# Whole-array matmuls for two heads at a time: values with 128 stationary columns, rotary keys on 128 rows

## The chip, the core and the metric

One core of a Trainium2 chip runs the whole program. The metric is the device time of one execution in microseconds. Five engines work side by side, each through its own queue in order: TensorE (PE; its weight loads are listed apart as PEld), VectorE (DVE), ScalarE (ACT), GpSimd (POOL) and SyncE (SP, which issues most DMAs). Matmul results land in PSUM, from where DVE and ACT read them.

## The reference, cut to what matters

Two blocks follow each other on 512 tokens of width 1024. The first block has two layers; each projects its input, runs three kinds of attention and projects back. The second has one layer with three mixers, then a feed-forward network. Four head groups matter here:

```python
# first block, per layer: forgetting heads (4 of width 64), stick-breaking heads (4 of width 64)
logits = s + cqb[..., :, None] - cum_logf[..., None, :]
p = jax.nn.softmax(jnp.where(causal, logits, -jnp.inf), axis=-1)
return jnp.einsum('bhqk,bhkd->bhqd', p.astype(v.dtype), v)
...
weights = jnp.where(strict, jnp.exp(jax.nn.log_sigmoid(z) + after), 0.0)
return jnp.einsum('bhqk,bhkd->bhqd', weights.astype(v.dtype), v)
...
yb = _from_blocks(ob) * jax.nn.silu(bg)      # and yc likewise

# second block: latent attention (4 heads; 128 plain and 64 rotary dimensions)
s = (jnp.einsum('bthd,bshd->bhts', qn, k_nope)
     + jnp.einsum('bthr,bsr->bhts', qp, k_pe)).astype(jnp.float32) * scale
```

The rotary keys `k_pe` are the same for all four heads.

## The kernel before, in words

A Python program writes all instructions; a scheduler then orders each engine's queue by priority. Side work (attention) and main work (projections of the next stage, with their weights loaded, split into two parts and multiplied three times in `mm3`, L212) are interleaved: a generator of attention steps is advanced some steps for each step of the projections (`merge`, L85). Attention steps have raised priority (`ahead`), their transposes and value matmuls lowered (`lag`).

Heads of width 64 are kept in pairs, `pr`, head `hh` of a pair on partitions 0 to 63 or 64 to 127. Projections leave 128 rows, two heads, in one tile; values `v[k]` hold, for key block k, 128 tokens on the rows and all heads' values side by side as columns, so the two heads of a pair are 128 adjacent columns.

Forgetting attention (`att_b`, L737) runs over pairs, then query blocks i of 128 (so i+1 key blocks), then the two heads. Each step makes scores, a masked minimum (`masked`, L720), an exponential and a scaling (`softmax`), and hands the rest to `step` (L1081) and the class `Steps`: one step later the weights are transposed on PE and copied by ACT, another step later `put` multiplies values and weights, one matmul group over the key blocks with the head's 64 value columns stationary and the 128 query columns moving, onto the head's 64 rows of the PSUM tile `pv`. `pv` has one buffer for the whole kernel (`PS`, L82); one tile serves a pair, and when both heads and all blocks are in it, `out_bc` (L558) multiplies it into the pair's gate with one DVE operation (L562).

Stick-breaking attention (`att_c`, L792) takes the heads in turn: `front` makes scores and logarithms, `sums` walks the key blocks from the last to the first and its `put` (L841) multiplies, with 64 value columns stationary and then 128 to 512 query columns moving (L847, L851). Again one `pv` serves a pair and one DVE operation (L564) takes it out.

Latent attention (`mla`, L1362) runs over query blocks and four heads. A score is a 128-row matmul (L1372) plus a rotary one (L1373) over 64 rows: queries of two heads lie on one tile's two halves, and the rotated keys `kpe`, made on rows 0 to 63 at L1220, are copied to rows 64 to 127 (L1221), so that each head finds keys on its own rows. In that part of the program tiles of 2 KB a row come from a set of 24 (`slot`, L67).

In the trace float32 matmuls stand as two instructions each, one after the other.

Of the kernel before, what the change touches and what calls it, by code (L numbers as in the profile page):

```python
# [15 lines left out]
ALU = mybir.AluOpType  # L16
# [4 lines left out]
P = 128  # L21
S = 512
NT = S // P
# [11 lines left out]
class Net:  # L35
# [471 lines left out]
    def layer1(self, l, hT, post, nxt):  # L507
# [5 lines left out]
        v, lf = self.vl  # L513
# [41 lines left out]

        oo, wait, last = {}, [], []

        def out_bc(k, pv, scale):  # L558

            g = gates[k]  # L560
            if scale == 1.0:
                nc.vector.tensor_mul(g, pv, g)  # L562
            else:
                nc.vector.scalar_tensor_tensor(g, pv, scale, g, op0=ALU.mult, op1=ALU.mult)  # L564
            finish(k, g)

        def finish(k=None, o=None):

# [168 lines left out]
    def att_b(self, bq, bk, v, lf, out, slot):  # L737
        nc = self.nc

        x = lf[:, :, 0:4]  # L740
        e = self.u("lfe", [P, NT, 4], 1)
        nc.scalar.activation(e, x, AF.Abs)
        nc.scalar.activation(e, e, AF.Exp, scale=-1.0)
        nc.scalar.activation(e, e, AF.Ln, bias=1.0)
        nc.vector.scalar_tensor_tensor(x, x, 0.0, e, op0=ALU.min, op1=ALU.subtract)
        nc.vector.tensor_copy(lf[:, :, 4:8], x)
        if not self.bounds:
            self.hgrn_bounds()
        nc.vector.tensor_copy(lf[:, :, 8:16], lf[:, :, 0:8])
        cumr = self.wa()  # L750
        nc.gpsimd.memset(cumr, 1.0)
        nc.gpsimd.affine_select(cumr, cumr, pattern=[[1, S]], compare_op=ALU.is_ge,
                                fill=0.0, base=0, channel_multiplier=-1)
        cum = self.p("s")
        for j in range(NT):
            nc.tensor.matmul(cum[0:16, j * P:], lhsT=lf[:, j, :], rhs=cumr[:, :S - j * P],
                             start=j == 0, stop=j == NT - 1)

        C, cu = self.sub.tile([P, S], F32R, name=self.nm("g"), tag="g", bufs=4), cum[0:16]
        nc.gpsimd.memset(C.bitcast(F32), 0.0)  # L760
        up = self.wa(dt=F32R)[0:16]
        sel = lambda k: self.sel[:, k:k + 1]
        nc.scalar.copy(up, cu)
        x = self.wa()[0:16]
        nc.vector.tensor_scalar_mul(x, up, sel(0))
        nc.vector.scalar_tensor_tensor(C[0:16], cu, sel(1), x, op0=ALU.mult, op1=ALU.add)
        yield
        steps = Steps(self)
        for pr in range(2):
            pv = self.p("pv")  # L770
            for i in range(NT):
                w = (i + 1) * P
                qi = slice(i * P, w)
                for hh in range(2):
                    h, r = pr * 2 + hh, hh * 64
                    sc = self.p("s")

                    n = max(w, 256)
                    self.dots(sc[:, :n], bq[pr][hh], bk[pr], hh, qi, slice(0, n))
                    scored = nc.tensor.matmul(sc[:, :n], lhsT=self.pick[:, h, :], rhs=C[:, :n], start=False, stop=True)  # L780
                    st = self.t("st", [P, 4], 6)
                    p = self.wa()
                    self.masked(p, sc, w, st[:, 1:2])
                    nc.scalar.activation(p[:, :w], p[:, :w], AF.Exp, bias=st[:, 1:2], scale=-1.0, accum_out=st[:, 2:3])
                    self.softmax(p, st, 0.5, w)
                    self.step(steps, scored, p, i, pv[r:r + 64, qi], lambda k, h=h: v[k][:, 512 + h * 64:576 + h * 64],
                              done=(lambda pr=pr, pv=pv: out(4 + pr, pv, 1.0)) if i == NT - 1 and hh else None)
                    yield
        steps.end()
        yield  # L790

    def att_c(self, cq, ck, v, out):  # L792
# [31 lines left out]
        pvs, puts = {}, []  # L824

        def sums(pr, hh, z, hi, lo):
            h, r = pr * 2 + hh, hh * 64
            for k in range(NT - 1, -1, -1):
                w = S - k * P

                sc = self.p("s")
                todo = [(self.ntri if j == k else self.nones, j, y) for j in range(k, NT) for y in (hi, lo)]
                for n, (m, j, y) in enumerate(todo):
                    wj = max(S - j * P, 256)
                    end = 128 + co[j] + S - j * P
                    last = nc.tensor.matmul(sc[:, S - wj:], lhsT=m, rhs=y[:, end - wj:end], start=n == 0, stop=n == len(todo) - 1)  # L836
                p = z[:, co[k]:co[k] + w]
                nc.vector.tensor_add(p, sc[:, k * P:], p)
                nc.scalar.activation(p, p, AF.Exp)

                def put(after, k=k, p=p, w=w):  # L841
                    if hh == 0 and k == NT - 1:
                        pvs[pr] = self.p("pv")
                    pv = pvs[pr]
                    vv = v[k][:, 768 + h * 64:832 + h * 64]
                    with self.lag():
                        x = nc.tensor.matmul(pv[r:r + 64, k * P:(k + 1) * P], lhsT=vv, rhs=p[:, :P], start=k == NT - 1, stop=False)  # L847
                        if after:
                            self.after(x, after)
                        if k < NT - 1:  # L850
                            nc.tensor.matmul(pv[r:r + 64, (k + 1) * P:], lhsT=vv, rhs=p[:, P:], start=False, stop=k == 0)  # L851
                    if hh and k == 0:
                        out(6 + pr, pv, 0.5)

                puts.append(put)
                if len(puts) > 1:
                    puts.pop(0)(last)
                yield
# [279 lines left out]
    def attention2(self, hT):  # L1138
# [67 lines left out]
        with self.tp("ph2m", "left") as mid:  # L1206
# [3 lines left out]
            with self.tp("ph2b", "right") as self.sub:  # L1210
# [7 lines left out]
                self.run_all(main((plist, "aq", 0, aq, -P ** -0.5), (plist, "aq", 256, aq, -P ** -0.5)))  # L1218
                self.run_all(low.second(qn, qp, kn, vc, tab, mslot))
                kpe = self.rope2_apply(kpr, 64, tab, self.slot())  # L1220
                nc.scalar.copy(kpe[64:128], kpe[0:64])  # L1221
            mxp = self.ctx2.enter_context(self.tp("ph2c", "right"))
            mx = [mxp.tile([P, S], F32, name=f"mx{c}", tag="mx", bufs=8) for c in range(8)]
            with self.tp("ph2d", "right") as self.sub:
# [137 lines left out]
    def mla(self, qn, qp, kn, kpe, vc, out):  # L1362
        nc = self.nc
        steps = Steps(self)
        for i in range(NT):
# [1 line left out]
            qi = slice(i * P, w)  # L1367
            pv = self.p("pv", [P, 4, P])
            for h in range(4):
                r = (h % 2) * 64  # L1370
                sc = self.p("s")
                nc.tensor.matmul(sc[:, :w], lhsT=qn[h][:, qi], rhs=kn[h][:, :w], start=True, stop=False)  # L1372
                scored = nc.tensor.matmul(sc[:, :w], lhsT=qp[h // 2][r:r + 64, qi], rhs=kpe[r:r + 64, :w], start=False, stop=True)  # L1373
                st = self.t("st", [P, 4], 6)
                p = self.wa()
                self.masked(p, sc, w, st[:, 1:2])
                nc.scalar.activation(p[:, :w], p[:, :w], AF.Exp, bias=st[:, 1:2], scale=-1.0, accum_out=st[:, 2:3])
                self.softmax(p, st, 0.5, w)
                self.step(steps, scored, p, i, pv[:, h, :], lambda k, h=h: vc[k][:, h * P:(h + 1) * P],
                          done=(lambda qi=qi, pv=pv: self.split_heads(out, qi, pv)) if h == 3 else None)  # L1380
                yield
# [448 lines left out]
```

## Time and profile before

| | |
|---|---|
| median of 3 runs | 1677.36 us (1676.02 to 1679.92) |
| the profiled execution | 1676.82 us |
| its span, first to last instruction | 1675.1 us |
| TensorE busy | 1618.9 us, 97% |
| VectorE busy | 1056.8 us, 63% |
| ScalarE busy | 734.6 us, 44% |
| GpSimd busy | 105.7 us, 6% |
| mean granted TensorE clock | 0.995 |

A row of the page's first part is an engine, its busy time, share of the span and number of instructions. Busy time of PE includes modelled ends, and its matmuls overlap: what one matmul costs is read from the start of one to the start of the next. A form such as `128*64 128x128` is rows by columns of the stationary operand, then the size of the moving one.

### The profile page before, as it was taken

The numbers are of one execution on the slowest core, as the hardware profiler recorded it, in microseconds if no ns is written. First come the engines' busy times: TensorE is split into PE (matmuls) and PEld (weight loads), VectorE is DVE, ScalarE is ACT, GpSimd is POOL, SyncE is SP. The second block draws the span as 40 slices with busy tenths as digits, with TensorE's granted clock in tenths as the row PEclk, the third lists the DMA queues.
The fourth block names the chain that finished last, engine by engine and source line by source line (L and its number), as shares of the span: only waits on it lengthen the run. The fifth ranks groups of instructions, "written<-read, shape, count | busy, mean of one in ns | idle before, by whom it ended". The sixth has DMA issues, their size and how long they took to land.

```text
span 1675.1 us, 24263 instructions
## 1 busy us (share of the span) xinstructions
PE 1618.9 (97%) x9320; PEld 1374.6 (82%) x9320; DVE 1056.8 (63%) x2281; ACT 734.6 (44%) x1507; POOL 105.7 (6%) x131
## 2 busy tenths in 40 slices
PE   6999999999999999899889999999999999999997
PEld 6878797987787889787778866788889988888997
DVE  7686779784578796747999995624355444343233
ACT  4455664443465643465443765522233222222222
POOL 1021000000000000002221001100000000000000
PEclk9999999999999999999999999999999999999999
DMA  7453032341121414332011320223432533333321
GB/s 229 141 167 109 26 116 74 101 152 51 51 76 39 148 55 126 121 100 64 26 30 49 93 76 27 91 91 108 144 120 101 176 101 101 101 101 95 95 90 62
DMA packets 141883, 160.06 MB, mean 96 GB/s; under 512 B 14100, under 2 KB 131108, under 8 KB 141256
## 3 DMA queue, kind: packets, MB, share of 16 engines
q1 hardware_dynamic: 135960, 141.34, 28.0%
q0 software_dynamic: 2944, 11.86, 2.1%
q10 hardware_dynamic: 2864, 5.32, 1.0%
q8 instruction: 73, 1.20, 0.3%
q14 instruction: 42, 0.34, 0.1%
HBM read 143.55 MB, written 15.21 MB: 95 GB/s over the span
## 4 chain that ended last, share of the span: by engine, by line
PE 76%; DVE 13%; ACT 3%; issue 2%; DMA 1%; POOL 1%; ACTq 0%; POOLq 0%
PE pj L217 18%; PE pj L218 18%; PE pj L216 18%; PE pv L1093 3%; PE s L216 2%; PE s L217 2%; PE s L218 2%; PE tr L731 2%; DVE wlo L203 2%; PE s L717 1%; PE s L836 1%; PE s L718 1%; DVE ixs L1313 1%; DMA wraw<-in_w_in_dram 1%; ACT whi L202 1%
## 5 line engine op out<-in xcount | busy, mean ns | idle before, releaser
L216 PE MATMUL pj<-hTh,whi 128*128 128x512 f32 (+1 forms) x1136 | 440.5, 388 | 0.0
L217 PE MATMUL pj<-hTl,whi 128*128 128x512 f32 (+1 forms) x1136 | 440.3, 388 | 0.0
L218 PE MATMUL pj<-hTh,wlo 128*128 128x512 f32 (+1 forms) x1136 | 439.8, 388 | 0.3 <-DVE wlo L203 0.3
L203 DVE TENSOR_TENSOR wlo<-wraw,whi 128x1024 fp32r<-128x1024 f32 (+3 forms) x237 | 271.9, 1153 | 240.1 <-ACT whi L202 236.3
L202 ACT CAST whi<-wraw 128x1024 fp32r<-128x1024 f32 (+3 forms) x237 | 229.1, 980 | 327.1 <-PE pj L217 193.5
L216 PEld LDWEIGHTS pj<-hTh,whi 128*128 128x128 f32 x1136 | 213.6, 188 | 45.4 <-issue 6.6
L217 PEld LDWEIGHTS pj<-hTl,whi 128*128 128x128 f32 x1136 | 213.6, 188 | 43.4 <-issue 4.7
L218 PEld LDWEIGHTS pj<-hTh,wlo 128*128 128x128 f32 x1136 | 213.6, 188 | 43.2 <-issue 3.8
L216 PE MATMUL pj<-whi,hTh 128*128 128x256 f32 (+2 forms) x352 | 101.1, 289 | 3.4 <-ACT whi L207 2.7
L218 PE MATMUL pj<-whi,hTl 128*128 128x256 f32 (+2 forms) x352 | 102.5, 292 | 0.0
L217 PE MATMUL pj<-wlo,hTh 128*128 128x256 f32 (+2 forms) x352 | 101.2, 288 | 0.0
L217 PE MATMUL pj<-wlo,t2k 128*128 128x256 f32 x304 | 85.9, 283 | 0.0
L218 PE MATMUL pj<-whi,t2k 128*128 128x256 f32 x304 | 85.7, 282 | 0.0
L216 PE MATMUL pj<-whi,t2k 128*128 128x256 f32 x304 | 85.3, 281 | 0.0
L216 PE MATMUL s<-whi,t2k 128*128 128x256 f32 x264 | 73.8, 280 | 0.0
L218 PE MATMUL s<-whi,t2k 128*128 128x256 f32 x264 | 73.8, 280 | 0.0
L217 PE MATMUL s<-wlo,t2k 128*128 128x256 f32 x264 | 73.8, 280 | 0.0
L216 PEld LDWEIGHTS pj<-whi,hTh 128*128 128x128 f32 x352 | 68.2, 194 | 5.1 <-ACT whi L207 3.3
L217 PEld LDWEIGHTS pj<-wlo,hTh 128*128 128x128 f32 x352 | 68.4, 194 | 0.5 <-DVE wlo L203 0.2
L218 PEld LDWEIGHTS pj<-whi,hTl 128*128 128x128 f32 x352 | 68.3, 194 | 0.4
L734 ACT COPY wa<-tr 128x128 f32<-128x128 f32 (+3 forms) x96 | 40.7, 424 | 58.8 <-PE tr L731 57.4
L722 DVE CUSTOM_DVE_ANT_0 wa<-s,mask 128x128 f32<-128x128 f32 (+3 forms) x112 | 52.5, 485 | 11.4 <-PE tr L731 7.9
(455 smaller groups left out, 3120.2 us busy)
## 6 DMA issues: line engine op xcount, KB each, us to landing
wraw<-in_w_in_dram SPq DMA_DIRECT2D x112, 512.0 KB, 3.8
wraw<-in_w_ffn_gate_dram SPq DMA_DIRECT2D x22, 512.0 KB, 3.9
wraw<-in_w_ffn_up_dram SPq DMA_DIRECT2D x22, 512.0 KB, 4.6
wraw<-in_w_ffn_down_dram SPq DMA_DIRECT2D x16, 512.0 KB, 3.6
tok<-hres SPq DMA_DIRECT2D x12, 512.0 KB, 7.7
wraw<-in_w_out_dram SPq DMA_DIRECT2D x12, 512.0 KB, 4.3
hres<-tok SPq DMA_DIRECT2D x12, 512.0 KB, 2.7
wraw<-in_w_out_dram SPq DMA_DIRECT2D x8, 384.0 KB, 3.0
```

What stands on the lines that cost most here:

```text
L202: nc.scalar.copy(hi[:, ka:kb], raw)
L203: nc.vector.tensor_sub(lo[:, ka:kb], raw, hi[:, ka:kb])
L216: nc.tensor.matmul(out, lhsT=wh(k), rhs=xh(k), start=start and k == 0, stop=False)
L217: nc.tensor.matmul(out, lhsT=wh(k), rhs=xl(k), start=False, stop=False)
L218: nc.tensor.matmul(out, lhsT=wl(k), rhs=xh(k), start=False, stop=stop and k == nk - 1)
L717: nc.tensor.matmul(sc, lhsT=stacked[:, rows], rhs=twice[hh][:, cols], start=True, stop=False)
L718: return nc.tensor.matmul(sc, lhsT=stacked[:, rows], rhs=twice[2 + hh][:, cols], start=False, stop=stop)
L722: self.nc.vector.tensor_tensor_reduce(p[:, :w], sc[:, :w], self.maskw[:, S - w:] if mask is None else mask, scale=1.0, scalar=3e38, op0=AL ...
L731: x = nc.tensor.transpose(pt[:, j, :], src[:, j * P:(j + 1) * P], self.ident)
L734: nc.scalar.copy(dst[:, :n, :], pt[:, :n, :])
L836: last = nc.tensor.matmul(sc[:, S - wj:], lhsT=m, rhs=y[:, end - wj:end], start=n == 0, stop=n == len(todo) - 1)
L1093: x = self.nc.tensor.matmul(out, lhsT=l, rhs=r, start=k == 0, stop=k == i)
```

## The change

Values: the 64-column stationary operand becomes the 128 columns of the pair, for each head. The result then has 128 rows, of which the head's own 64 are kept. Because both heads now write all rows, each head has a `pv` tile of its own: the loop of forgetting attention runs heads outside and query blocks inside, and `out_bc` is called per head on its 64 rows; the pair is finished after the second.

Rotary keys: two tiles in place of one, the keys on rows 0 to 63 with zeros below, and the keys on rows 64 to 127 with zeros above; the rotary matmul takes all 128 rows of the queries' tile, so the other head's queries meet zeros.

```diff
-        def out_bc(k, pv, scale):
+        def out_bc(k, hh, pv, scale):
 
-            g = gates[k]
+            r = slice(hh * 64, hh * 64 + 64)
+            g = gates[k][r]
             if scale == 1.0:
-                nc.vector.tensor_mul(g, pv, g)
+                nc.vector.tensor_mul(g, pv[r], g)
             else:
-                nc.vector.scalar_tensor_tensor(g, pv, scale, g, op0=ALU.mult, op1=ALU.mult)
-            finish(k, g)
+                nc.vector.scalar_tensor_tensor(g, pv[r], scale, g, op0=ALU.mult, op1=ALU.mult)
+            if hh:
+                finish(k, gates[k])
...
         for pr in range(2):
-            pv = self.p("pv")
-            for i in range(NT):
-                w = (i + 1) * P
-                qi = slice(i * P, w)
-                for hh in range(2):
-                    h, r = pr * 2 + hh, hh * 64
+            vv = lambda k, c=512 + pr * P: v[k][:, c:c + P]
+            for hh in range(2):
+                h = pr * 2 + hh
+                pv = self.p("pv")
+                for i in range(NT):
+                    w = (i + 1) * P
+                    qi = slice(i * P, w)
...
-                    self.step(steps, scored, p, i, pv[r:r + 64, qi], lambda k, h=h: v[k][:, 512 + h * 64:576 + h * 64],
-                              done=(lambda pr=pr, pv=pv: out(4 + pr, pv, 1.0)) if i == NT - 1 and hh else None)
+                    self.step(steps, scored, p, i, pv[:, qi], vv,
+                              done=(lambda pr=pr, hh=hh, pv=pv: out(4 + pr, hh, pv, 1.0)) if i == NT - 1 else None)
...
                 def put(after, k=k, p=p, w=w):
-                    if hh == 0 and k == NT - 1:
+                    if k == NT - 1:
                         pvs[pr] = self.p("pv")
                     pv = pvs[pr]
-                    vv = v[k][:, 768 + h * 64:832 + h * 64]
+                    vv = v[k][:, 768 + pr * P:896 + pr * P]
                     with self.lag():
-                        x = nc.tensor.matmul(pv[r:r + 64, k * P:(k + 1) * P], lhsT=vv, rhs=p[:, :P], start=k == NT - 1, stop=False)
+                        x = nc.tensor.matmul(pv[:, k * P:(k + 1) * P], lhsT=vv, rhs=p[:, :P], start=k == NT - 1, stop=False)
...
-                            nc.tensor.matmul(pv[r:r + 64, (k + 1) * P:], lhsT=vv, rhs=p[:, P:], start=False, stop=k == 0)
-                    if hh and k == 0:
-                        out(6 + pr, pv, 0.5)
+                            nc.tensor.matmul(pv[:, (k + 1) * P:], lhsT=vv, rhs=p[:, P:], start=False, stop=k == 0)
+                    if k == 0:
+                        out(6 + pr, hh, pv, 0.5)
...
                 kpe = self.rope2_apply(kpr, 64, tab, self.slot())
-                nc.scalar.copy(kpe[64:128], kpe[0:64])
+                kpe = kpe, self.slot()
+                nc.scalar.copy(kpe[1][64:128], kpe[0][0:64])
+                nc.gpsimd.memset(kpe[0][64:128], 0.0)
+                nc.gpsimd.memset(kpe[1][0:64], 0.0)
...
-                scored = nc.tensor.matmul(sc[:, :w], lhsT=qp[h // 2][r:r + 64, qi], rhs=kpe[r:r + 64, :w], start=False, stop=True)
+                scored = nc.tensor.matmul(sc[:, :w], lhsT=qp[h // 2][:, qi], rhs=kpe[h % 2][:, :w], start=False, stop=True)
```

## Rows read from the trace of the kernel before

**Rows 1.** The page's first part: engine, busy us, share, instructions.

```profile
PE 1618.9 (97%) x9320; PEld 1374.6 (82%) x9320; DVE 1056.8 (63%) x2281; ACT 734.6 (44%) x1507; POOL 105.7 (6%) x131
```

**Rows 2.** Stretches: us; PE, PEld, DVE, ACT, POOL busy; clock; DMA share, GB/s.

```profile
85.00:131.00 46.00, 45.53 (x252) 34.93 (x252) 36.93 (x106) 23.35 (x58) 12.46 (x20) 1.00 0.54 182
155.00:212.00 57.00, 57.00 (x288) 42.97 (x288) 45.03 (x84) 39.67 (x77) 1.04 (x6) 1.00 0.13 37
408.00:450.00 42.00, 42.00 (x234) 31.47 (x234) 25.01 (x74) 22.86 (x55) 1.47 (x2) 1.00 0.16 43
988.00:1028.00 40.00, 39.77 (x170) 23.11 (x169) 27.74 (x92) 17.83 (x54) 3.31 (x4) 1.00 0.12 34
```

**Rows 3.** Changed lines: count, ns min/median/max, first and last start, forms.

```profile
L1093 PEld LDWEIGHTS pv<-wa,v x160: 132/137/137, 90.6 to 448.9; 128*64 128x64 f32 x160
L1093 PEld LDWEIGHTS pv<-wa,t2k x80: 186/192/247, 998.6 to 1038.4; 128*128 128x128 f32 x80
...
L847 PE MATMUL pv<-cz,v x64: 272/298/323, 161.5 to 531.5; 128*64 128x128 f32 x64
...
L1373 PE MATMUL s<-t2k,ms x32: 272/481/693, 991.1 to 1025.9; 64*128 64x128 f32 x8, 64*128 64x256 f32 x8, 64*128 64x384 f32 x8, 64*128 64x512 f32 x8
```

**Rows 4.** PE in order of time, forgetting attention: start us, us, line, operands, shapes, count.

```profile
113.21 0.38 PE L731 MATMUL tr<-ident,wa 128*128 128x128 f32 x2
113.52 0.43 PE L1093 MATMUL pv<-wa,v 128*64 128x128 f32 x2
...
114.22 0.39 PE L216 MATMUL pj<-hTh,whi 128*128 128x512 f32 x1
```

**Rows 5.** PE in order of time, latent attention: values on the whole array.

```profile
998.78 0.39 PE L1093 MATMUL pv<-wa,t2k 128*128 128x128 f32 x2
...
999.24 0.40 PE L218 MATMUL pj<-hTh,wlo 128*128 128x512 f32 x1
...
1016.04 0.38 PE L731 MATMUL tr<-ident,wa 128*128 128x128 f32 x2
1016.26 0.61 PE L1093 MATMUL pv<-wa,t2k 128*128 128x128 f32 x4
```

**Rows 6.** PE in order of time, stick-breaking attention, around one value group.

```profile
162.87 0.39 PE L217 MATMUL pj<-hTl,whi 128*128 128x512 f32 x1
163.09 0.40 PE L218 MATMUL pj<-hTh,wlo 128*128 128x512 f32 x1
...
164.34 0.28 PE L717 MATMUL s<-lt,lt 128*128 128x256 f32 x1
```

**Rows 7.** PE in order of time, later attention: twelve whole-array value matmuls.

```profile
1060.77 1.51 PE L1093 MATMUL pv<-wa,av 128*128 128x128 f32 x12
```

**Rows 8.** PE in order of time, latent attention, around one head's rotary scores.

```profile
1024.41 0.59 PE L1372 MATMUL s<-ms,t2k 128*128 128x512 f32 x1
...
1024.85 0.59 PE L1372 MATMUL s<-ms,t2k 128*128 128x512 f32 x1
...
1026.42 0.33 PE L731 MATMUL tr<-ident,wa 128*128 128x128 f32 x1
1026.59 0.28 PE L1093 MATMUL pv<-wa,t2k 128*128 128x128 f32 x1
```

**Rows 9.** The output operation of forgetting attention; its own wait; who waited for it.

```profile
L562 DVE TENSOR_TENSOR g<-pv,g x4: 687/692/693, 110.2 to 449.3; 128x512 f32<-128x512 f32 x4
...
  PE pv L1093: 5.1, 3
...
  PEld pv L1093: 0.4, 1
```

**Rows 10.** GpSimd: a memset, and its queue before the bias additions.

```profile
L760 POOL MEMSET g<- x2: 528/536/543, 35.9 to 328.3; 128x512 f32 x2
...
989.78 3.36 POOL L1350 TENSOR_TENSOR bs<-bs,mask 128x128 f32<-128x128 f32 x4 [92.58 <-DMA bs<-bias]
```

**Rows 11.** The split of weights on DVE, all of it.

```profile
L203 DVE TENSOR_TENSOR wlo<-wraw,whi x237: 680/1220/2545, 9.1 to 1647.9; 128x1024 fp32r<-128x1024 f32 x93, 128x768 fp32r<-128x768 f32 x13, 128x512 fp32r<-128x512 f32 x12, 128x1040 fp32r<-128x1040 f32 x1
```

More of the change, by code (lines that the diff above doesn't have):

```diff
@@ L826, in sums @@
         def sums(pr, hh, z, hi, lo):
-            h, r = pr * 2 + hh, hh * 64
             for k in range(NT - 1, -1, -1):
@@ L1369, in mla @@
             for h in range(4):
-                r = (h % 2) * 64
                 sc = self.p("s")
                 nc.tensor.matmul(sc[:, :w], lhsT=qn[h][:, qi], rhs=kn[h][:, :w], start=True, stop=False)
-                scored = nc.tensor.matmul(sc[:, :w], lhsT=qp[h // 2][r:r + 64, qi], rhs=kpe[r:r + 64, :w], start=False, stop=True)
+                scored = nc.tensor.matmul(sc[:, :w], lhsT=qp[h // 2][:, qi], rhs=kpe[h % 2][:, :w], start=False, stop=True)
                 st = self.t("st", [P, 4], 6)
```

## The prediction

> **What bounds the kernel now.** I read the page's busy line first, then busy time in the stretches that the diff touches, then the instructions of the changed lines in order of time. TensorE is busy 1618.9 of 1675.1 us, VectorE 1056.8 [rows 1]. The stretches show the same more sharply: in 85 to 131 us (forgetting attention, layer 0) PE is busy 45.53 of 46.00, in 155 to 212 (stick-breaking attention) 57.00 of 57.00, in 408 to 450 (forgetting attention, layer 1) 42.00 of 42.00, in 988 to 1028 (latent attention) 39.77 of 40.00, all at a granted clock of 1.00 [rows 2]. PE executes in order and the attention steps are interleaved with projections, so in these stretches time is what PE's queue costs, instruction by instruction. A busy PE is not a PE at its peak, though: what has to be read is the distance from one start to the next.
>
> **What the odd shapes cost.** The matmuls that change use part of the array: 128\*64 for the values (160 loads, and so matmuls, in `step`, 64 in L847 and as many pairs' second halves in L851) and 64\*128 for the rotary half of the latent scores (32) [rows 3]. Nearly everything else is 128\*128.
>
> Values, forgetting heads: two transposes start at 113.21, the two value matmuls at 113.52, then a projection matmul, and the next at 114.22 [rows 4]. So two transposes take 0.31, and two value matmuls with one projection 0.70. The same sequence on the whole array, in later attention: two transposes 0.22 (1016.04 to 1016.26), two value matmuls and one 512-column projection 0.46 (998.78 to 999.24) [rows 5]. The excursion into the half-width shape costs 0.09 on the way in and 0.24 on the way out: 0.33 us.
>
> Values, stick-breaking heads: a 512-column projection matmul starts 0.22 after the one before it. From 163.09 one of these, four value matmuls and one 512-column sum take until 164.34, 1.25 us [rows 6]. On the whole array that is 0.22, plus the 0.46 of above, plus two more value matmuls at 0.112 (the spacing in a run of twelve whole-array ones, which lasts 1.51 us from first start to last end, the last by itself 0.28 [rows 7, 8]), together 0.90. Excess 0.35.
>
> Rotary scores: at 512 columns a whole-array score matmul occupies 0.43 (1024.41 to 1024.85). From 1024.85 that second one, two 64-row ones and one transpose take until 1026.59, 1.74 us [rows 8]. With whole-array spacing: 3 x 0.43 + 0.11 = 1.40. Excess 0.34.
>
> So the three places agree on about 0.33 us for each trip out of and back into the 128\*128 shape, independent of how long the trip is. That is the quantity the change removes.
>
> **How many trips.** By the loops, forgetting heads: 2 layers x 4 heads x 4 query blocks = 32 groups. Stick-breaking: 2 x 4 x 4 key blocks = 32. Latent: 4 blocks x 4 heads = 16. In the order on the chip two neighbours share one trip twice (a run of sixteen value matmuls, a run of four rotary ones), so 78. Gross gain 78 x 0.33 = 25.7 us, from about 31, 32 and 15 trips.
>
> **What the new form costs on PE.** Moving columns are unchanged, and rows of zeros or unused columns add none, so matmul time is unchanged. Loads grow from 64 to 128 columns: 0.137 to 0.192 us each [rows 3]. I put this at nothing, because loads run under the matmul ahead: with 0.192 loads the run of twelve still advances every 0.112 us [rows 7]. The cover is that overlap; if it failed, 272 loads x 0.055 = 15.0 us come back. The Trainium skill ("TensorE: Matmul & The Clock Gate", section "LDWEIGHTS (loading the stationary operand)") speaks against the change here: it makes a load's time depend on the stationary columns and not on the rows. The trace agrees on the load itself, and the sum with it exposed would be 10.7 us of gain instead of 25.7; the spacing in the run of twelve decides for the larger one.
>
> **The output operation and its buffer.** Before, one DVE operation per pair took both heads' result from PSUM, 0.692 us on 128x512 [rows 9]. Now each head has its own, on 64 rows. 64x512 is as many columns, so I keep 0.69: 8 more operations (2 layers x 2 pairs x 2 kinds), 5.5 us of DVE time. They are not on PE's path by themselves; I charge a fifth, 1.1, with ends 0 and 5.5. The single `pv` buffer is now handed over between the two heads of a pair as well. In forgetting attention that is 2 more per layer, 4 in all: the first value matmul of the second head waits for the first head's DVE operation, and queued behind it on PE are the next scores, transposes and projections. The trace shows the present handovers: DVE stood 5.1 us in three waiting for the last value matmul, PE stood once for 0.4 us waiting for DVE [rows 9]. I take 0.4 for each new one, 1.6; the upper end is DVE's wait and operation exposed, 1.7 + 0.69, so 9.6. In stick-breaking attention the next head's scores and logarithms lie between, so 0. The loop order in forgetting attention (head outside, block inside) moves no work into or out of the stretch and issues no DMA: 0.
>
> **What is late next.** Without the trips PE needs less in each stretch, and DVE more. 85 to 131: 46 - 15 x 0.33 = 41 against 36.9 + 1.4 = 38.3 of DVE, 93%, where it was 80%. 155 to 212: 51.7 against 46.4, 90%, and the same in layer 1. 408 to 450: 36.7 against 26.4. 988 to 1028: 35 against 27.7 [rows 2]. So PE stays the longer one everywhere, but in the first stretch and the two stick-breaking ones (47 trips, 15.5 us) VectorE comes close, and its operations arrive in bunches. I charge a fifth of that gain, 3.1, with ends 0 and half, 7.8.
>
> **The rotary keys.** One more 2 KB buffer (by my count of live tiles 24 of 24: 4+4+4 values and queries, 8 of the mixer's output, keys, raw keys, the two new ones), two memsets of 64x512 on GpSimd, and the ScalarE copy that was there already now goes to the other tile. A 128x512 memset took 0.54 [rows 10]. GpSimd stood 92.58 us idle before its bias additions at 989.78 [rows 10], and the zero rows depend on nothing, so I put them at nothing. If they were queued behind those additions the first scores would wait up to 3.4.
>
> **Sum.** 25.7 - 1.1 - 1.6 - 3.1 = 19.9 us. The profiled execution took 1676.8 (span 1675.1 plus 1.7 around it), so 1656.9; the median of the runs shown is 0.5 above that execution, so 1657.4.
>
> **Rivals.** (a) VectorE catches up: handovers and bunching at their upper ends, 25.7 - 9.6 - 1.1 - 7.8 - 0 = 7.2 of gain, 1670.2; between this and the forecast the middle is 1664. For it: 93% and 90% above, and DVE's standing for PE. Against it: PE stood still for nothing in 155 to 212 and 408 to 450 [rows 2]. (b) Loads exposed: 10.7 less the other charges of 5.8, 4.9 of gain, 1672.5. Against it: the run of twelve. (c) The change doesn't do what it says: the 0.33 belongs not to the shape but to going from projections to values, and stays: 1677.4 + 2.7 of new charges, 1680, or no difference. Against it: the latent and later heads' whole-array values sit between the same neighbours and don't pay it. (d) Slower: the handover of the one `pv` buffer stops PE. Place: the second head's first value matmul, eight times (forgetting and stick-breaking). Price: the last value matmul 0.28, two weight subtractions ahead in DVE's queue, one of the longest and one median, 2.5 and 1.2 [rows 11], and the output operation 0.69: 4.7 each, 37.6, less 25.7, so 1689.3. It decides from 25.7 / 8 = 3.2 us per handover; the one wait seen is 0.4.
>
> **How the numbers follow.** Forecast (gain of 14 to 26) 0.74; (a) 0.14; (b) 0.04; (c) 0.04; (d) 0.04. About 0.2%, 3.4 us, is what a measurement of this kernel can tell from no change. (a) and (b) are faster by more, (c) mostly within, (d) slower: faster 0.92, same 0.04, slower 0.04. Range: the low end is the gross gain with nothing charged, 1651.7, and as the order that the scheduler writes will shift a little, 1651; the high end takes in most of (a), 1667.
>
> **What would show it.** Right: all matmuls of L1093, the two lines in `put` and the rotary line read 128\*128; two value matmuls and one projection take 0.46 instead of 0.70, and two transposes ahead of them 0.22; PE's matmul count is unchanged; stretches of about 5 us less each; DVE has 8 more output operations of 0.69. Wrong: value matmuls of the new form spaced over 0.15 (loads exposed); PE waits for the output operation of more than 1 us each; PE idle for DVE in 85 to 131 or 155 to 212 growing by more than 8 us; first scores at 991 waiting for GpSimd.

## The result, and the profile after

| | before | after |
|---|---|---|
| median | 1678.44 us (4 runs, 1676.02 to 1679.92) | 1660.97 us (4 runs, 1657.93 to 1661.98) |
| the profiled execution (span) | 1676.82 us (1675.1) | 1657.93 us (1656.0) |
| ratio after / before | | 0.9894, interval 0.9876 to 0.9913 |

The kernel is 17.5 us faster; 19.9 were forecast, and 1657.4 us. Run again on another chip it took 1661.55 us beside 1676.01, a ratio of 0.9914 (0.9900 to 0.9927), 14.5 us faster.

The first part of the page of after, as in [rows 1]: PE is 20.4 us less busy with the same 9320 matmuls, and DVE has eight instructions more.

```profile
PE 1598.5 (97%) x9320; PEld 1377.6 (83%) x9320; DVE 1060.2 (64%) x2289; ACT 735.2 (44%) x1507; POOL 105.8 (6%) x133
```

The changed lines of after, columns as in [rows 3]. All are 128\*128 now. A load for values takes 0.19 us where it took 0.137, and a matmul itself lasts what it lasted.

```profile
L1096 PEld LDWEIGHTS pv<-wa,v x160: 186/192/246, 87.0 to 441.6; 128*128 128x128 f32 x160
L1096 PE MATMUL pv<-wa,v x160: 270/275/377, 87.1 to 441.7; 128*128 128x128 f32 x160
...
L850 PE MATMUL pv<-cz,v x64: 270/274/377, 157.6 to 514.1; 128*128 128x128 f32 x64
...
L1379 PE MATMUL s<-t2k,ms x32: 272/432/593, 978.3 to 1008.1; 128*128 128x128 f32 x8, 128*128 128x256 f32 x8, 128*128 128x384 f32 x8, 128*128 128x512 f32 x8
```

PE in order of time in after, three groups that answer to [rows 4], [rows 6] and [rows 8]: forgetting, stick-breaking and latent attention.

```profile
402.73 0.38 PE L733 MATMUL tr<-ident,wa 128*128 128x128 f32 x2
402.95 0.39 PE L1096 MATMUL pv<-wa,v 128*128 128x128 f32 x2
403.09 0.47 PE L217 MATMUL pj<-hTl,whi 128*128 128x512 f32 x1
403.40 0.40 PE L218 MATMUL pj<-hTh,wlo 128*128 128x512 f32 x1
...
158.94 0.40 PE L218 MATMUL pj<-hTh,wlo 128*128 128x512 f32 x1
159.17 0.39 PE L850 MATMUL pv<-cz,v 128*128 128x128 f32 x2
159.40 0.39 PE L854 MATMUL pv<-cz,v 128*128 128x128 f32 x2
159.56 0.50 PE L839 MATMUL s<-ch,ntri 128*128 128x512 f32 x1
159.91 0.28 PE L719 MATMUL s<-lt,lt 128*128 128x256 f32 x1
...
1003.54 1.02 PE L1378 MATMUL s<-ms,t2k 128*128 128x512 f32 x2
1004.40 1.02 PE L1379 MATMUL s<-t2k,ms 128*128 128x512 f32 x2
1005.26 0.38 PE L1096 MATMUL pv<-wa,t2k 128*128 128x128 f32 x2
```

Two transposes take 0.22 us (402.73 to 402.95; it was 0.31), two value matmuls and one projection 0.45 (402.95 to 403.40; it was 0.70). The stick-breaking group takes 0.97 (158.94 to 159.91) where it took 1.25. Two plain and two rotary scores take 1.72 (1003.54 to 1005.26), 0.43 each. Matmuls of the new form mostly lie 0.112 us apart, as whole-array ones did in [rows 7], so the longer loads are hidden.

Where the time went: both traces cut at the same work (first score of forgetting attention, first sum of stick-breaking, last value of the attention behind it, and so on). Columns as in [rows 2]. First before, then after; left out are the stretches that the diff doesn't touch, but for the first.

```profile
0.00:84.50 84.50, 70.44 (x384) 60.48 (x385) 57.73 (x156) 39.34 (x81) 9.99 (x25) 0.98 0.60 184
84.50:159.60 75.10, 74.63 (x382) 58.95 (x382) 53.48 (x130) 36.85 (x80) 17.03 (x27) 1.00 0.45 146
159.60:319.10 159.50, 158.25 (x933) 131.86 (x932) 133.00 (x327) 92.01 (x197) 8.28 (x16) 1.00 0.25 78
...
406.80:482.30 75.50, 75.50 (x384) 58.92 (x384) 41.35 (x101) 37.16 (x80) 5.47 (x7) 1.00 0.20 57
482.30:641.00 158.70, 157.18 (x931) 131.55 (x929) 132.73 (x327) 92.02 (x197) 8.27 (x16) 1.00 0.27 82
...
981.00:1027.70 46.70, 46.47 (x199) 28.63 (x200) 34.32 (x105) 22.86 (x62) 3.31 (x4) 1.00 0.14 39
```

```profile
0.00:82.40 82.40, 68.33 (x384) 58.08 (x385) 57.65 (x156) 39.34 (x81) 9.99 (x25) 1.00 0.61 189
82.40:155.80 73.40, 71.97 (x382) 58.73 (x382) 54.61 (x132) 37.18 (x80) 16.98 (x27) 1.00 0.46 149
155.80:311.60 155.80, 154.23 (x933) 133.39 (x932) 133.93 (x329) 92.11 (x197) 8.26 (x16) 1.00 0.26 80
...
399.20:471.60 72.40, 71.74 (x385) 59.57 (x385) 43.03 (x103) 37.27 (x80) 5.46 (x7) 1.00 0.21 59
471.60:627.10 155.50, 154.20 (x932) 133.41 (x931) 133.91 (x329) 91.84 (x197) 8.26 (x16) 1.00 0.27 84
...
966.60:1009.70 43.10, 43.00 (x199) 31.31 (x200) 33.94 (x105) 23.15 (x62) 2.42 (x4) 0.96 0.14 42
```

Forgetting attention became shorter by 1.7 and 3.1 us in the two layers, stick-breaking with the attention behind it by 3.7 and 3.2, latent attention by 3.6: 15.3 us. In the repetition on the other chip the same five stretches became 17.1 us shorter, 4.9 of it in the latent one. Its rows for the stretch ahead of latent attention, where only the copy and the memsets of the rotary keys are changed, and for the latent one:

```profile
627.90:970.30 342.40, 317.82 (x1901) 276.40 (x1899) 276.30 (x551) 179.17 (x400) 40.44 (x20) 0.99 0.26 73
970.30:1012.10 41.80, 41.66 (x198) 30.02 (x199) 33.95 (x105) 22.96 (x62) 3.33 (x4) 1.00 0.15 44
```

The stretch ahead took 342.4 us here, 340.0 in before and 339.5 in after; 825.3 to 828.8 was granted a clock of 0.51 here, and the trace of before has no such drop at that work. With 2.4 us lost there this execution is 16.0 us shorter than that of before in all. The first stretch has no changed instruction either, and its 2.1 us in after are the clock's: 0.98 of full speed in the one execution, 1.00 in the other. So the change itself brings 15 to 17 us, and of the 19.1 between the two spans some is chance.

### The profile page after: what moved, and what is told of

The parts are those of the page before. It is cut to its first block, busy times and chain, and to the rows that moved or that the text cites. A ratio compares the mean times of both kernels' runs of the same rounds, so it can differ in the third digit from the quotient of the medians.

```text
span 1656.0 us, 24283 instructions
## 1 busy us (share of the span) xinstructions
PE 1598.5 (97%) x9320; PEld 1377.6 (83%) x9320; DVE 1060.2 (64%) x2289; ACT 735.2 (44%) x1507; POOL 105.8 (6%) x133
## 3 DMA queue, kind: packets, MB, share of 16 engines
q10 hardware_dynamic: 2864, 5.32, 1.0%
## 4 chain that ended last, share of the span: by engine, by line
PE 75%; DVE 15%; ACT 3%; issue 2%; POOL 1%; DMA 1%; ACTq 0%; POOLq 0%; DVEq 0%
PE pj L217 18%; PE pj L218 18%; PE pj L216 18%; PE pv L1096 3%; PE s L218 2%; PE s L217 2%; PE s L216 2%; DVE wlo L203 2%; PE tr L733 2%; PE s L719 1%; DVE ixs L1320 1%; PE s L720 1%; PE s L839 1%; DVE E L1678 1%; DVE wa L724 1%
## 5 line engine op out<-in xcount | busy, mean ns | idle before, releaser
L203 DVE TENSOR_TENSOR wlo<-wraw,whi 128x1024 fp32r<-128x1024 f32 (+3 forms) x237 | 271.9, 1153 | 241.9 <-ACT whi L202 238.2
```

Source lines behind the costliest of these rows:

```text
L203: nc.vector.tensor_sub(lo[:, ka:kb], raw, hi[:, ka:kb])
```

## Experiments

The table is worked out from the traces of before, after and eight of the runs below, in their order: in each stretch, PE's distances from start to start less the fastest spacings seen (0.109 us for a 128-column value or transpose matmul, 0.43 for 512 columns of latent scores, 0.223 for 512 of a projection), so what PE loses there, in us. "Next" is the attention that follows stick-breaking; "order only" is the kernel with the old shapes in the new order, "old order" the one with the new shapes in the old.

```
            before after  forg. stick rotary order  old   two   ScalarE  ScalarE
                          only  only  only   only  order  outs  +GpSimd  only
forgetting 0  7.30  5.57  5.49  7.27  7.29   6.96  5.43   7.26   7.12    5.32
stick-br.  0  7.73  3.42  7.73  3.42  7.74   8.80  3.38  10.34   6.31    3.11
next       0  6.21  6.86  6.41  6.87  6.28   7.82  6.79   6.66   6.76    6.93
forgetting 1  7.22  4.01  4.05  7.24  7.23   7.40  4.04   6.70   4.63    4.19
stick-br.  1  7.74  3.38  7.74  3.38  7.75   8.88  3.37  10.34   6.28    3.08
next       1  5.75  6.64  5.76  6.72  5.78   7.86  6.67   6.81   6.82    6.85
latent        7.30  3.64  7.03  7.01  2.74   8.54  3.59   7.25   2.42    3.62
sum          49.25 33.52 44.21 41.91 44.81  56.26 33.27  55.36  40.34   33.10
```

**One part at a time.** Three kernels with only the forgetting heads' values, only the stick-breaking heads' values, only the rotary keys in the new form; the rest is that of before. The edit of the second, seen from before:

```diff
-                    vv = v[k][:, 768 + h * 64:832 + h * 64]
+                    vv = v[k][:, 768 + pr * P:896 + pr * P]
```

> Only the forgetting heads' values take the pair's 128 columns (head outside, one output operation per head); stick-breaking and rotary matmuls as before. Theory (each trip out of the 128*128 shape costs PE 0.33 us): 31 trips, 10.2 us, less what the changed kernel's trace shows lost there to the handover of the single PSUM buffer and to other waits (PE's excess over its columns fell by 1.7 us in layer 0 and 3.2 in layer 1): 4 to 7 us faster than before. Rival (the gain comes from order and buffers, not from shape): 0 to 2 us.

> Only the stick-breaking heads' values take the pair's 128 columns, with one output operation per head. Theory of the trips: 32 trips of 0.33 us, 10.6 us, less small waits: 8 to 10.5 us faster than before, and as the handover falls into the next head's scores, nothing lost to it. Rival (VectorE, 80% busy there, catches up): 3 to 5 us.

> Only the rotary half of the latent scores goes over 128 rows, keys padded with zeros. Theory of the trips: 15 trips of 0.33 us, 5 us, none lost: 4 to 5.5 us faster than before. Rival (a stretch in which the softmax chain sets the pace): 1 to 2 us. If the gains add up, this one and the two others give 17 to 18 us.

Measured beside 1677.65 of before: 1673.28 (ratio 0.9973, 0.9962 to 0.9984), 1669.00 (0.9948, 0.9935 to 0.9961) and 1670.62 (0.9965, 0.9952 to 0.9978), so 4.4, 8.7 and 7.0 us faster, in or above the ranges that the theory of the trips gave (by the table, stick-breaking's 7.3 lies below its 8 to 10.5). By the table the parts bring 5.0, 7.3 and 4.4 us, 16.8 together, about what the whole change brings (15.7): the gains add up and don't take from one another. Rotary keys alone do better in time than in their own stretch. In the two profiled executions (spans 1675.1 and 1668.5) the rest is the clock's chance: the first stretch, ahead of any changed instruction, took 82.3 us at a clock of 1.00 where before took 84.5 at 0.98. The two profiled executions of the changed kernel differ there in the same way (82.4 and 84.0). The stick-breaking column shows a price paid later: 8.7 us less in its own stretches, 0.7 and 1.0 more in the attention behind them.

The rotary kernel is also the cleanest test of the shape: PE, ScalarE and VectorE carry out the same operations in the same order as in before, and only GpSimd has its two memsets more. Its latent stretch (columns as in [rows 2]) took 42.1 us, at a clock of 1.00 as in before, where it was 46.7. By the table that is 4.6 us less, 0.30 for each of the 15 trips.

```profile
978.50:1020.60 42.10, 41.73 (x198) 30.02 (x199) 33.92 (x105) 22.83 (x62) 3.30 (x4) 1.00 0.15 43
```

**Order, buffers and output operations without the shapes.** The changed kernel with the old 64-column values and 64-row keys.

```diff
-                    self.step(steps, scored, p, i, pv[:, qi], vv,
+                    self.step(steps, scored, p, i, pv[r:r + 64, qi], lambda k, h=h: v[k][:, 512 + h * 64:576 + h * 64],
...
-                    vv = v[k][:, 768 + pr * P:896 + pr * P]
+                    vv = v[k][:, 768 + h * 64:832 + h * 64]
```

> Order, buffers and output operations of the change (head outside, one PSUM tile and one output operation per head) with the old shapes: 64 columns, 64 rows. Theory: the trips stay, the charges come: 1 to 4 us slower than before. Rival (order and buffers bring the gain): 5 us or more faster than before.

Measured: 1683.63 (1.0034, 1.0021 to 1.0047), 6.0 us slower than before, more than either theory gave. Its loss stands in the stick-breaking stretches and behind them (1.1 to 2.1 each) and in the latent one (1.2, where its code is that of before, but the granted clock was 0.96 in place of 1.00), while the forgetting stretches, where the new loop order is, are about as before (6.96 and 7.40). Against this kernel the change of shapes alone is worth 22.7 us by the table (56.26 less 33.52), and as much by the medians. The new order makes neighbours share a trip, 70 remain here, so 0.32 us for each; since the two kernels' queues differ at the end of stick-breaking too, this isn't a clean price.

**Is the price graded?** The first head of each pair with 96 of the 128 columns, the even heads' keys with 96 of the 128 rows.

```diff
-                    vv = v[k][:, 768 + pr * P:896 + pr * P]
+                    n = 128 if hh else 96
+                    vv = v[k][:, 768 + pr * P:768 + pr * P + n]
```

> The changed kernel, but the first head of each pair takes 96 of the 128 value columns in stick-breaking attention, and even heads 96 of the 128 rows in the rotary scores. Theory (the cost hangs on leaving the whole array's shape, and 96 of 128 is still that shape): these groups start 0.11 or 0.23 after the instruction ahead and are left without excess, as at 128. Rival (the cost grows with the unused part): an excess of 0.1 to 0.2 us at each group of 96, none at 128.

One execution: 1660.53 us. The queues of all engines have the order of the changed kernel. The kernel with 96 columns, its value line (columns as in [rows 3]), then PE in order of time around the group that was shown of after at 158.94:

```profile
L851 PEld LDWEIGHTS pv<-cz,v x64: 159/174/193, 159.0 to 515.0; 128*96 128x96 f32 x32, 128*128 128x128 f32 x32
...
160.52 0.39 PE L218 MATMUL pj<-hTh,wlo 128*128 128x512 f32 x1
160.75 0.38 PE L851 MATMUL pv<-cz,v 128*96 128x128 f32 x2
160.96 0.38 PE L855 MATMUL pv<-cz,v 128*96 128x128 f32 x2
161.16 0.50 PE L839 MATMUL s<-ch,ntri 128*128 128x512 f32 x1
161.50 0.28 PE L719 MATMUL s<-lt,lt 128*128 128x256 f32 x1
```

The group takes 0.98 us, as with 128 columns (0.97), though the operand is no longer 128 wide. With 96 rows of keys the latent stretch took 41.8 us, as with all rows in the repetition of the changed kernel on this chip. So what cost 0.33 is the 64-wide form and not an operand short of 128: three quarters of the array is as free as all of it.

**The changed kernel again, and with a raised priority for its output operations.**

```diff
-            if scale == 1.0:
-                nc.vector.tensor_mul(g, pv[r], g)
...
+            with self.tc.high_priority(3 * HP):
+                if scale == 1.0:
+                    nc.vector.tensor_mul(g, pv[r], g)
...
```

> The changed kernel again, as the reference for the next one on the same chip: 17 to 18 us faster than before.

> The changed kernel with its output operations scheduled ahead of other VectorE work. Theory: PE's two waits for the output operation in layer 0 (0.6 and 0.43 us idle, 1.9 with what follows) go, 1 to 2 us faster than the changed kernel. Rival (the waits are moved, since VectorE does the same work): within 0.5 us of it.

Measured beside 1676.01: 1661.55 and 1661.69 (0.9914 and 0.9910). The priority hardly changed the order: VectorE's differs from that of the changed kernel in one place (at 437.7 us an output operation changes places with a reciprocal), those of PE and ScalarE don't differ, and PE stands as long for the output operations (1.1 us in two waits; 1.0 in after). So this run is one more repetition, and whether output operations ahead of other work would help isn't tested.

**The old loop order.** The changed kernel with query blocks outside and heads inside, `pv` tiles of two blocks for both heads, so four 64x256 output operations for a pair.

```diff
-            for hh in range(2):
-                h = pr * 2 + hh
-                pv = self.p("pv")
-                for i in range(NT):
...
+            for i in range(NT):
...
+                if i % 2 == 0:
+                    pv = self.p("pv", [P, 2, 256])
+                for hh in range(2):
...
```

> The changed kernel with the forgetting heads' old loop order (query block outside, head inside): the PSUM tile of a pair holds both heads' 128-row results of two query blocks, and four output operations of 64x256 take each pair out (two after blocks 0 and 1, two after 2 and 3). Whole-array shapes everywhere, so no trips. Theory (what forgetting attention lost, 5 of 10 us, is mostly the head-outside order and its handover): 2 to 4 us faster than the changed kernel, that is 17 to 20 faster than before; PE's excess over its columns in the two stretches falls below 5.5 and 4.0. Rival (lost to VectorE being late whatever the order; now 8 smaller output operations per layer and three handovers): within 1 us of the changed kernel, or slower.

Measured 1659.84 beside 1677.30 (0.9899, 0.9884 to 0.9914): the changed kernel's time. The forgetting stretches lose as much (5.43 and 4.04), only by other waits.

**Two output operations in the kernel before.**

```diff
-            g = gates[k]
-            if scale == 1.0:
-                nc.vector.tensor_mul(g, pv, g)
...
+            for r in (slice(0, 64), slice(64, 128)):
+                g = gates[k][r]
+                if scale == 1.0:
+                    nc.vector.tensor_mul(g, pv[r], g)
...
```

> The kernel before, with each pair's output operation cut in two of 64x512, one per head, at the same place; shapes, order and buffers as before. 8 more VectorE operations of 0.69 us. Theory (they are not on the path by themselves): 0 to 1.5 us slower than before. Rival (the charge seen with the old shapes in the new order, 5 us, is these operations): 4 to 6 us slower.

Measured 1682.76 (1.0029, 1.0018 to 1.0040), 5.5 us slower. What PE waited for in 150 to 225 of this kernel (us in all, times, longest); the same rows stand in 470 to 550:

```profile
PE s L718 <- DVE t2k L711: 1.1, 2, 0.9
PE pj L216 <- ACT whi L202: 0.8, 1, 0.8
PE pj L216 <- DVE wp L535: 0.3, 1, 0.3
```

In before PE stands there once, for 0.3 us. PE waits for none of the operations of 0.69 us themselves, and still a layer loses 2.6 us where stick-breaking ends: behind the last one stand the rotary steps and the weight split that PE needs next. But the scheduler also wrote another order. When the last output operation of layer 0 starts, VectorE has done 22 weight subtractions (L203) in before and in the changed kernel, and 20 here. So the 2.6 us are the price of the operations and of this order together, and the run doesn't part them. In the changed kernel the first head's operation runs long before that point, and PE stands there for 0.3 and 0.2 us.

**The output operations off VectorE.** ScalarE copies the values out, GpSimd multiplies them into the gate; on the changed kernel, and on the one with the old loop order.

```diff
-            if scale == 1.0:
-                nc.vector.tensor_mul(g, pv[r], g)
...
+            x = self.wa()[r]
+            nc.scalar.mul(x, pv[r], scale)
+            nc.gpsimd.tensor_mul(g, x, g)
```

> The changed kernel with every output operation of the forgetting heads taken off VectorE: ScalarE copies (and scales) the head's values from PSUM into an SBUF tile, GpSimd multiplies them into the gate. Theory (VectorE is what is late in this attention, and gives back about half of the 10.2 us that the 31 whole-array groups should bring there): 16 operations of 0.68 us leave VectorE, its waits ahead of the step's values go, PE's excess in the forgetting stretches falls from 5.4 and 4.0 us to below 4.5 and 3.2, and the kernel is 1 to 5 us faster than the changed one, 18 to 22 us faster than before. Rival (ScalarE, which issues its exponentials in order, and the hop to GpSimd make the PSUM buffer as late as VectorE did): within 1 us of the changed kernel, or slower.

> The same (output operations by ScalarE and GpSimd) on the kernel with the forgetting heads' old loop order and whole-array values, four output operations of 64x256 for a pair. Theory (VectorE's lateness): 1 to 5 us faster than the changed kernel, excess in the forgetting stretches below 4.5 and 3.2 us. Rival: within 1 us of the changed kernel, or slower, with PE's waits now on ScalarE's operations.

Measured beside 1676.71: 1667.32 (0.9946, 0.9932 to 0.9961) and 1670.91 (0.9963, 0.9950 to 0.9976), about 6 and 9 us slower than the changed kernel. The first of them, GpSimd and VectorE in order of time at the end of stick-breaking, and the wait of PE that follows:

```profile
203.85 1.61 POOL L564 TENSOR_TENSOR g<-wa,g 64x512 f32<-64x512 f32 x1
...
202.88 0.42 DVE L711 CAST t2k<-t2k 64x512 fp32r<-64x512 f32 x1
203.34 0.98 DVE L710 SCALAR_TENSOR_TENSOR t2k<-wp,t2k 64x512 fp32r<-64x512 f32 x1
204.35 1.39 DVE L711 CAST t2k<-t2k 64x512 fp32r<-64x512 f32 x1
...
205.89 0.48 PE L718 MATMUL s<-t2k,t2k 128*128 128x256 f32 x2 [1.22 <-DVE t2k L711]
```

The same cast on VectorE took 0.42 us at 202.88 and 1.39 at 204.35, beside GpSimd's product of 203.85 to 205.46 (in the changed kernel, without that product, the second cast took 0.59), and PE stood 1.22 for it. So this kernel doesn't test the theory: it takes work off VectorE and slows what is left. The Trainium skill ("SBUF — State Buffer", section "SBUF: two separate sides") says that VectorE and GpSimd share one pair of ports and that one holds it for its whole instruction; the two casts fit that.

**ScalarE alone.** The changed kernel with ScalarE writing the values straight to the gate's tile: this leaves out the product with the gate, and nothing is added on GpSimd.

```diff
-            if scale == 1.0:
-                nc.vector.tensor_mul(g, pv[r], g)
...
+            nc.scalar.mul(g, pv[r], scale)
```

> The changed kernel with all 16 output operations of the forgetting and stick-breaking heads (0.69 us each) taken off VectorE and nothing put on GpSimd: ScalarE copies the head's values, scaled, straight into the gate's tile. This leaves out the product with the gate. Theory (these operations on VectorE, 11 us in all, are what kept the change from its gross gain): PE's excess in the forgetting stretches falls from 5.4 and 4.0 us to below 4.5 and 3.2, the end of stick-breaking stays at 3.4, and the kernel is 1 to 5 us faster than the changed one, 18 to 22 us faster than before. Rival (what is lost there is the order in which scores, maxima, exponentials and transposes of one step follow each other; any other placing of the output operation shifts that order without shortening it): within 2 us of the changed kernel or slower, and the waits ahead of transposes and scores stay.

Measured 1661.12 beside 1677.14 (0.9912, 0.9898 to 0.9926): the changed kernel's time again, and 6 us better than with GpSimd's products. The line that replaces the output operation, and who waited for it (us, times):

```profile
L562 ACT ACTIVATE g<-pv x16: 591/593/595, 106.6 to 514.5; 64x512 f32<-64x512 f32 x16
...
  PE pv L1093: 0.9, 1
```

Without any output operation VectorE is no longer in PE's way at the handover, but ScalarE is, for 0.9 us; the forgetting stretches lose 5.32 and 4.19, against 5.57 and 4.01 in after. So these operations' time on VectorE is not what ate the gain; what they cost in another place, here on ScalarE, isn't excluded.

## Why the prediction was right, point by point

**The price of a trip.** Right in kind and in size. Around each value group of the traces, the starts exceed whole-array spacing by 6.09 us in a layer's 16 stick-breaking groups of before and by 0.93 in after: 0.32 a group, where 0.33 was read. For layer 1's 16 forgetting groups it is 5.50 and 0.92, 0.29 each; for layer 0's 15 it is 5.19 and 2.25, of which 1.03 is waiting, so 0.26 each. These lower figures don't come from cheaper trips: 24 of the 31 forgetting groups of before exceed by 0.35 or 0.36, the one of [rows 4] among them, and most groups of after by 0.01 to 0.03. What pulls them down are gaps that a few groups of after keep (0.29 and 0.28 in layer 1; in layer 0 two with 0.4 to 0.5 beyond their waits), and two groups of before that cost less (0.23 and 0.08). One count was misread on the way: L851 has 48 loads and not 64; the sum of 272 loads has it right. The Trainium skill ("TensorEngine Tiling (Array Packing)", section "Key Properties") says that a change of the array's tiling mode drains TensorE; the trace agrees, 128\*64 and 64\*128 cost on the way in and out, 128\*96 and 96\*128 don't, and it gives that drain its size, about 0.3 us for both ways.

**The loads.** Right: 0.19 us each, and no spacing grew. Rival (b) is out, and so is (c), since the same neighbours now pass without the excess, in the rotary kernel with the order of before on PE unchanged.

**The buffer's handover.** Near in size (1.6 forecast, 1.03 measured), wrong in its spread. The one present wait of 0.4 us, from which the 1.6 was made, was a weight load's (PEld in [rows 9]); no value matmul of before stood for it. PE's waits in 82 to 130 of after, whole; then the first of the two handovers in order of time:

```profile
PE s L719 <- DVE t2k L712: 1.5, 2, 1.1
PE pv L1096 <- DVE g L563: 1.0, 2, 0.6
```

```profile
106.10 0.68 DVE L549 SCALAR_TENSOR_TENSOR g<-g,pj 128x512 f32<-128x512 f32 x1
...
107.14 0.68 DVE L563 TENSOR_TENSOR g<-pv,g 64x512 f32<-64x512 f32 x1
...
107.88 0.94 PE L1096 MATMUL pv<-wa,v 128*128 128x128 f32 x6 [0.60 <-DVE g L563]
```

The output operation starts behind the gate's own step (L549, here the first of its 16, which makes the gate that the operation multiplies into, so no order could put it ahead), PE stands 0.60 us for its end, and the second time 0.43; in layer 1 and in stick-breaking it doesn't stand at all. That is 0 to 0.6 for each, far from the 3.2 at which rival (d) would have decided.

**VectorE late.** Here the sizes were wrong. Forecast: 1.1 for the eight operations and 3.1 for lateness in the first forgetting stretch and the stick-breaking ones. With the handovers the charges were 5.8 us; the five stretches became 15.3 to 17.1 us shorter, so 8.6 to 10.4 of the gross 25.7 did not arrive. The sign that I had named, stretches of about 5 us less each, wasn't met: 1.7 to 3.7, and 4.9 only in the latent one of the repetition. Split by part, gross and arrived (after; second chip): forgetting 10.2 and 4.8 (5.2), stick-breaking 10.6 and 6.9 (7.0), latent 5.0 and 3.6 (4.9). Latent attention, to which I charged nothing, gave all of it where the clock stayed at full; in the trace of after it was granted 0.96 in that stretch.

Of the 5.4 us missing in forgetting attention, 1.0 is the handover, 1.7 the gaps left beside value groups (8.5 arrived for the 31 trips), and about 2.7 are small waits and gaps before scores and transposes. Layer 1 lost as well, which I had held for safe since VectorE has room there: PE waits there for the masked minimum. Its row in 395 to 475 of after:

```profile
PE s L719 <- DVE st L724: 0.6, 1, 0.6
```

These gaps came back in other places with the old loop order, and stayed with no output operation on VectorE (PE again stands 0.6 us for the minimum in 395 to 475), so neither that operation's time on VectorE nor the loop order alone is their cause. That it is the chain of score, minimum, exponential and transpose itself, which no longer fits under less PE time, is the reading that is left; no run shortened that chain, and it stays open.

Of the 3.7 us missing in stick-breaking, 0.3 are gaps left beside value groups, 1.5 come back as a loss in the attention behind it (+0.65 and +0.89 in the table), and 1.7 go to gaps elsewhere in its own stretch (trips 5.2 a layer, stretch 4.3 and 4.4). What causes those 1.7 wasn't separated. The eight extra operations, with the order that the scheduler writes for them, can be dear, 5.5 us in the kernel before, but only from the end of that stretch on, where the changed kernel has one operation and that kernel two in a row. What they cost in the changed kernel wasn't measured by itself; with none on VectorE it was no faster, so nothing speaks for more than the fifth that I charged, but my argument for it (off PE's path) left out that place.

**Rotary keys, GpSimd.** Right: the first rotary scores wait for nothing of GpSimd, whose instructions went from 131 to 133.

**The total.** 25.7 less 5.8 was forecast, 25.7 less about 9.5 came in the stretches; by the medians the gain was 17.5 us, and 14.5 on the other chip, where 19.9 were forecast. The mis-sized term is the lateness: with the output operations it was put at 4.2 us, and at nothing in layer 1's forgetting attention, and 7.6 to 9.4 us besides the handover did not arrive; what makes them, VectorE or the chain of each step, stays open. The profiled execution, 1657.93 us, met 1656.9 partly by the 2.1 us of its first stretch, which is luck. The range held the mis-sized term because its high end was put at 1667; rival (a) reached from 1664 to 1670.2, so that took in about half of it, not most.

## What to carry to other kernels

A single 64-wide matmul group among whole-array ones costs about 0.3 us, as long as a run of three 128-column values; computing the neighbour's columns too, or multiplying zeros, is free where loads are hidden. Count such trips in the order on the chip and price them by starts, on several groups of each kind. Then expect less than the sum where the engine was nearly full: here 60 to 67% of it arrived, about half in forgetting attention, since shorter matmul time uncovers waits in the same stretch and in the next.

## What the runs showed of the hardware

- An operand of 96 columns costs no more between 128-wide neighbours than a whole one (0.98 and 0.97 us for the same group), nor does one of 96 rows (41.8 us for the latent stretch with either); a 64-wide one does (1.25 us for the group).
- VectorE's 64x512 cast took 0.42 us alone and 1.39 beside a GpSimd product of 1.61. Giving GpSimd work to relieve VectorE made the kernel 6 us slower than giving it to ScalarE alone (1667.32 and 1661.12 us), though the second also leaves out the products.
- TensorE's granted clock can differ between two executions of one kernel at the same place. In after, PE was busy 1.55 of 3.40 us from 964.0 to 967.4 at a clock of 1.00, and was then granted 0.51, near the lower level of 1.2 GHz, from 967.4 to 970.9. In the repetition PE was busy 1.64 of 3.50 us at that place and kept 1.00 behind it. The latent stretch took 43.1 and 41.8 us. Likewise from 34.0 to 37.5 us, before any changed instruction, before was granted 0.54 (PE busy 1.25 of the 2.00 us ahead of it, at 1.00) and after 1.00 (1.56 of 2.00). Such stretches near half speed move a single execution by 1 to 2 us, as much as some of the effects asked about here.
